# Part one of a streaming conformer layer: the order in which VectorE, ScalarE and GpSimd issue, and the lag before one attention head

## The chip, the cores and the metric

The kernel runs on one core of a Trainium2 chip. TensorE (PE) multiplies matrices, VectorE (DVE), ScalarE (ACT) and GpSimd (POOL) do the work on vectors, and SyncE (SP) issues most of the transfers between the chip's memory and the on-chip buffers. Each engine works through its own list of instructions, one after the other, and an instruction that waits for a semaphore holds everything behind it on that engine. The metric is the time of one execution on the device in microseconds; lower is better.

## The reference

One layer of a streaming encoder for 2048 prompt rows and 64 sample rows of width 1024:

```python
h = rms_norm(x, g1) * (1 + sc1) + sh1          # sc1, sh1, ... from silu(c) @ w_ada
z = h @ w_in                                    # glu_a | glu_b | q | k | v | two gates
u = glu_a * sigmoid(glu_b)
y = silu(layer_norm(causal_depthwise_conv(u, 31 taps) + b_dw))
conv_out = y @ w_conv_out
q, k = rms_norm(q per head), rms_norm(k per head)
o = softmax(q k^T / 8 + rel_bias, band of 9 chunks of 64) v      # 8 heads of 64
merged = sigmoid(g_conv) * conv_out + sigmoid(g_attn) * (o @ w_attn_out)
x = x + gt1 * (merged @ w_o)
x = x + gt2 * ffn(rms_norm(x, g2) * (1 + sc2) + sh2)             # SwiGLU, width 2816
```

The outputs are the new rows of prompt and sample, the last rows of the convolution's input, and the last k and v rows.

## The kernel before

The work is in two parts. Part one makes everything up to the attention's output and the gates; part two merges the two branches, adds the residual and does the feed-forward network. Only part one is touched here. It goes over the 2112 rows in four blocks (0 to 576 with the sample rows, then three of 512), and for each block through the stages in `ORDER`: q, first quarter of the convolution (GLU and taps), k, second quarter, v, third and fourth quarter, gates. A product in float32 precision is made as three matmuls of a high and a low half (`mm3`), so most operands exist twice: ACT rounds the high half (`whi`, `hh`, `ph`, `part_h`), DVE or POOL subtracts it to get the low half (`wlo`, `hl`, `pl`, `part_l`).

Beside the main stage, other work is fed in by a planner. Each piece (a block's conv-norm, a quarter's 31 taps, a tile's input norm, a head of attention) is a Python generator in a `Lane`; a `Meter` around every engine adds an estimate of each instruction's duration to that engine's load, and after each product `stream.spend()` lets lanes whose due time has come emit their next step. A step yields the load at which its inputs should be there. So the program's text order, as emitted, already is a plan for every engine. Which of it the chip sees is settled afterwards: the framework's scheduler puts each engine's instructions in an order of its own, except on the engines that are named in `tc.manual_schedule(...)`, which issue in the emitted order. Before, that was PE alone, from the end of the first block's opening products (`first_block`) to `ordered.close()` at the end of part one. Transfers that SP issues are in nobody's fixed list, so the scheduler places them in both kernels.

Every instruction of PE, DVE, ACT and POOL goes through `Meter.run`, so nearly all rows of the profile say L105 and are told apart by the names of their tiles:

- A head of attention (`attend`): `sc` (scores, PE, in one pair of PSUM banks), `pr,sm<-sc,bias` (score and maximum, DVE; the maximum is read by a following row `sm`), exp and scale of `pr` (ACT), transposes `ptp` (PE), `ph` (ACT) and `pl` (DVE), product with the values `po` (PE), `other` (ACT) and `o32_p` (DVE; the profile shortens it to `o_p`). The first block interleaves each prompt head with a head of the sample rows.
- Outputs kept as two halves (`parts()`): tiles `part_h` and `part_l`, two buffers each, shared by q and k after their norms, by conv-norm (`c_d`) and by attention output (`o_d`). A buffer comes free when the transfer that stores it has landed.
- Conv-norm of a block (`conv_norm`): POOL multiplies `y<-y,s`, ACT makes tanh `ln<-y,lnh`, DVE scales `y` and `ln`, then `part_h`, `part_l` and the two stores to `c_d`, four times per block of rows.
- q and k rows (`qk_rows`): `sq`, `kn` (ACT), `ssq`, `t` (DVE), `r` (POOL), `kn<-kn,r` (DVE), then transposes and `part_h`, `part_l`.

`fetch(i)` loads what head number i needs: q and k (`q2`, `kk`, one buffer each, so a head's load waits for the last scores of the head before) and the bias of the head. The head's first scores are due when the load meter of PE has moved on by a lag: `QK_LAG` = 9000 or, for a head that follows another kind of head, `FIRST_LAG` = 14000 ns. In each block the order of heads is 0 to 7; the heads of the first block are of kinds 0 and "s" in turn, those of the others of kind 1, 2 or 3.

Of the kernel before, what the change touches and what calls it, by code (L numbers as in the profile page):

```python
# [622 lines left out]
def streaming_layer(ctx: ExitStack, tc: tile.TileContext, I, O):  # L623
# [481 lines left out]
    def cached_kv():  # L1105
        rows_ = [(src, j) for j in range(CACHE // P) for src in (ck, cv)]
        ts = []
        for i, (src, j) in enumerate(rows_):
            for src_, j_ in rows_[len(ts) : i + 2]:
                t = temp("cache")  # L1110
                nc.sync.dma_start(t, src_[j_ * P : (j_ + 1) * P])
                ts.append((t, stream.load["pe"] + CACHE_LAG))
            t, landed = ts[i]
            yield landed
            if src is ck:
                store_kq(t, P, k_d, j * P)
            else:
                store_v(t, P, j * P)
            yield
# [349 lines left out]
    def load_bias(h):  # L1469
        for r in (0, HD):  # L1470
            nc.sync.dma_start(
                bias[r : r + HD, HD - r : 640 - r],
                bass.AP(tensor=rb_d.tensor, offset=rb_d.offset + 768 * h + HD, ap=[[1, HD], [1, 576]]),
            )
        return bias

    ahead_qk, spare = {}, {"open": False, "heads": []}
    order, loaded, now = [], {}, {"scored": -1, "finished": -1, "bias": None}
# [8 lines left out]
    def fetch_qk(i):  # L1487
        if i < len(order) and ("qk", i) not in now:
            x, h = order[i]
            if spare["open"]:  # L1490
                spare["heads"].append(i)
            now["qk", i] = load_qk(x, h, *spans(x))

    def fetch(i):
        if i < len(order) and i not in loaded:
            x, h = order[i]
            fetch_qk(i)
            if now["bias"] is None or now["bias"][0] != h:
                now["bias"] = h, load_bias(h)
            first = x != "s" and (not i or order[i - 1][0] not in (x, "s"))  # L1500
            lag = FIRST_LAG if first else QK_LAG
            loaded[i] = max(stream.load["pe"] + BIAS_LAG, ahead_qk.get(i, stream.load["pe"] + lag))

# [5 lines left out]
    def attend(i):  # L1509
        x, h = order[i]  # L1510
        q0, nq, k0, nk = spans(x)
        yield lambda: now["scored"] == i - 1
        fetch(i)
        fetch_v(i)
        if not i:
# [7 lines left out]
        for t in range(0, nq, P):  # L1523
            n = min(P, nq - t)
            if x not in (0, "s"):
                ps = ps_a.tile([P, 2, 512], F32, tag="s", name="sc")
                for j in range(2):
                    for d in range(2):
                        pe.matmul(ps[:, j, :320], q2[:, d, t : t + P], kk[:, t + 320 * j : t + 320 * j + 320], start=d == 0, stop=d == 1)
                w, src, bs = 640, ps[:, :, :320], bias[:, ::-1]  # L1530
            else:
                w = nk if x == "s" else t + P

                if "banks" not in now:
                    sc = ps_a.tile([P, 2, 512], F32, tag="s", name="sc")
                    now["banks"] = [sc[:, 0:1], sc[:, 1:2]]
                ps = now["banks"].pop(0)
                now["banks"].append(ps)
                for d in range(2):
                    pe.matmul(ps[:n, 0, :w], q2[:, d, t : t + n], kk[:, :w], start=d == 0, stop=d == 1)  # L1540
                src, bs = ps[:n, 0:1, :w], bias[:n, 64:384][:, ::-1] if x == "s" else bias[:, :w][:, ::-1]
            pr, sm, free, ready = softmax_max(src, n, w, bs)
            tiles.append((pr, sm, n, w))
            if t + P < nq:
                yield free + PE_LAG, SCORE_ROOM
            else:
                fetch(i + 1)
                if (x, order[min(i + 2, len(order) - 1)][0]) in ((0, 0), ("s", "s")):
                    fetch_qk(i + 2)
                now["scored"] = i  # L1550
            if t:
                softmax_scale(*tiles[-2], x in ON_ACT)
# [86 lines left out]
    W = Weights((nc.sync, act, dve, gps), wpool, dram, stream, list(weight_order()), source, 3, 5, lambda key: key[0] in KEPT)  # L1639
    first_block(xs)  # L1640
    ordered = ExitStack()
    ordered.enter_context(tc.manual_schedule(engines={mybir.EngineType.PE}))
    norm_lane.add(cached_kv())
    mods = mod_steps()
    norms = {}
# [734 lines left out]
```

## Time and profile before

| | |
|---|---|
| time, median of three runs | 2958.93 us (2955.85 to 2965.5) |
| the profiled execution's own time | 2957.35 us |
| its span, first to last instruction | 2955.5 us |
| mean granted TensorE clock | 0.995 |
| first block's opening products | 0 to 97 us |
| the stretch that the change can reorder | 97 to about 1181 us |
| part two | about 1181 to 2955.5 us |

In the rows that follow, a timeline row has the start and the duration in us, the engine, the operation with its tiles, and in brackets how long the engine was idle just ahead of it and who ended that. In a table by windows each engine has its busy time and, in parentheses, its number of instructions; then come the granted TensorE clock (1.00 is full speed), the busy share of the sixteen DMA engines and the bytes moved per time.

### The profile page before, as it was taken

To read this page: it belongs to the slowest core of one execution; us is meant where nothing else is said; L and a number is where in the kernel's file an instruction comes from. 1 tells how busy PE (TensorE), PEld (TensorE's weight loads), DVE (VectorE), ACT (ScalarE), POOL (GpSimd) and SP (SyncE) were. 2 spreads that over 40 slices of the span, in tenths; PEclk is the share of its full clock that TensorE was granted. 3 is DMA by queue.
4 is the path that set the end of the run, shared out by engine and by line. 5 is a ranking of instruction groups with operands and counts; after the bars stand their busy time and mean duration, and the time that the engine had idled before them with its cause. 6 is when DMAs were issued, how large, how long until landed. Compare 5 with 4: busy or idle time off the path is not lost.

```text
span 2955.5 us, 44837 instructions
## 1 busy us (share of the span) xinstructions
PE 2892.0 (98%) x16193; PEld 2586.7 (88%) x16193; DVE 2049.8 (69%) x3648; ACT 1364.3 (46%) x2453; POOL 1161.4 (39%) x753
## 2 busy tenths in 40 slices
PE   7999999999999999999999999999999999999999
PEld 5899777887888788888999998999999999999998
DVE  5897787668857885477777756666666547566666
ACT  3345533661465267464334345444444345444442
POOL 1101210111011102454666452366667742465767
PEclk9999999999999999999999999999999999999999
DMA  9989899878996897985444876232333965333333
GB/s 320 312 297 309 274 283 324 269 229 294 285 313 209 294 264 239 290 298 171 147 147 143 268 257 227 93 120 91 114 122 104 331 225 185 97 99 108 115 106 126
DMA packets 467067, 628.04 MB, mean 212 GB/s; under 512 B 36196, under 2 KB 314584, under 8 KB 466845
## 3 DMA queue, kind: packets, MB, share of 16 engines
q1 hardware_dynamic: 452944, 606.11, 63.4%
q10 hardware_dynamic: 13901, 19.08, 1.9%
q8 instruction: 127, 2.08, 0.3%
q14 instruction: 95, 0.78, 0.1%
HBM read 476.53 MB, written 148.54 MB: 211 GB/s over the span
## 4 chain that ended last, share of the span: by engine, by line
PE 46%; DVE 2%; DMA 2%; ACT 1%; issue 1%; POOL 1%; SPq 0%; ACTq 0%; DVEq 0%; POOLq 0%
PE ps L105 28%; PE pd L105 13%; PE pw L105 5%; DVE wlo L105 1%; DMA cin<-o_d 1%; ACT whi L105 1%; POOL wlo L105 0%; DMA tg<-g_d 0%; DVE ps L105 0%; ACT xn L105 0%; DMA wst<-in_w_ffn_in 0%; DMA wfo<-in_w_ffn_out 0%; DVE acc L105 0%; DVE sums L105 0%; PE pt L105 0%
## 5 line engine op out<-in xcount | busy, mean ns | idle before, releaser
L105 PE MATMUL ps<-t,whi 128*128 128x384 f32 (+1 forms) x2112 | 501.9, 322 | 3.2 <-DVE u L105 1.1
L105 POOL TENSOR_TENSOR wlo<-wst,whi 128x1024 fp32r<-128x1024 f32 (+1 forms) x159 | 362.7, 2293 | 233.7 <-ACT whi L105 195.6
L105 ACT ACTIVATE whi<-wst 128x1024 fp32r<-128x1024 f32 (+1 forms) x265 | 258.2, 979 | 316.5 <-PE ps L105 127.1
L105 PE MATMUL ps<-b,whi 128*128 128x384 f32 (+1 forms) x1584 | 380.6, 325 | 5.4 <-DVE v L105 2.1
L105 PEld LDWEIGHTS ps<-t,whi 128*128 128x128 f32 x2112 | 367.8, 188 | 10.6 <-ACT u L105 3.1
L105 DVE SCALAR_TENSOR_TENSOR y<-u,wd,y 128x512 f32<-128x512 f32 (+1 forms) x480 | 370.1, 773 | 7.5
L105 PE MATMUL ps<-hh,whi 128*128 128x512 f32 (+2 forms) x992 | 363.4, 366 | 0.1
L105 DVE TENSOR_TENSOR acc<-acc,pd 128x512 f32<-128x512 f32 x482 | 322.3, 685 | 48.7 <-PE pd L105 46.0
L105 PE MATMUL ps<-hh,wlo 128*128 128x512 f32 (+2 forms) x992 | 345.6, 348 | 0.3 <-DVE wlo L105 0.3
L105 PE MATMUL ps<-hl,whi 128*128 128x512 f32 (+2 forms) x992 | 345.2, 348 | 0.0
L105 PE MATMUL ps<-t,wlo 128*128 128x384 f32 (+1 forms) x1056 | 338.2, 321 | 0.0
L105 PE MATMUL pd<-whi,hid 128*128 128x512 f32 x912 | 297.5, 391 | 0.3 <-DVE hid L105 0.3
L105 PEld LDWEIGHTS ps<-b,whi 128*128 128x128 f32 x1584 | 276.8, 188 | 13.6 <-DVE v L105 3.2
L105 ACT ACTIVATE pr<-pr,sm 128x640 f32<-128x640 f32 (+2 forms) x272 | 202.1, 749 | 153.9 <-DVE sm L105 150.9
L105 PE MATMUL ps<-b,wlo 128*128 128x384 f32 (+1 forms) x792 | 256.0, 323 | 0.0
L105 POOL TENSOR_TENSOR r<-t,mhalf 128x1 f32<-128x1 f32 (+2 forms) x68 | 82.4, 1219 | 414.8 <-DVE t L105 375.0
L105 PEld LDWEIGHTS ps<-hh,wlo 128*128 128x128 f32 x992 | 187.3, 189 | 23.3 <-DVE wlo L105 0.5
L105 DVE TENSOR_TENSOR wlo<-wst,whi 128x1024 fp32r<-128x1024 f32 (+1 forms) x106 | 135.7, 1284 | 99.2 <-ACT whi L105 98.2
L105 PEld LDWEIGHTS ps<-hh,whi 128*128 128x128 f32 x992 | 187.7, 189 | 18.0 <-issue 2.9
L105 PEld LDWEIGHTS pd<-whi,hid 128*128 128x128 f32 x912 | 171.1, 188 | 36.5 <-DVE acc L105 0.8
L105 PEld LDWEIGHTS ps<-hl,whi 128*128 128x128 f32 x992 | 188.1, 190 | 14.5 <-issue 1.7
L105 PEld LDWEIGHTS ps<-t,wlo 128*128 128x128 f32 x1056 | 198.0, 188 | 0.8
(233 smaller groups left out, 6299.1 us busy)
## 6 DMA issues: line engine op xcount, KB each, us to landing
whi<-w_din_h SPq DMA_DIRECT2D x72, 512.0 KB, 5.2
wlo<-w_din_l SPq DMA_DIRECT2D x72, 512.0 KB, 7.8
wst<-sum_d SPq DMA_DIRECT2D x131, 256.0 KB, 2.9
wfo<-in_w_ffn_out SPq DMA_DIRECT2D x64, 512.0 KB, 4.1
wmod<-in_w_ada SPq DMA_DIRECT2D x46, 512.0 KB, 9.1
sum_d<-ws SPq DMA_DIRECT2D x88, 256.0 KB, 2.2
wst<-in_w_ffn_in SPq DMA_DIRECT2D x85, 256.0 KB, 3.2
wst<-in_w_in SPq DMA_DIRECT2D x40, 512.0 KB, 7.2
```

What stands on the lines that cost most here:

```text
L105: self.last = f(*args, **kw)
```

## The change

Two things. `fetch` gives the longer lag also to the first head of the block of kind 1, which follows the last sample head; before, only kinds 2 and 3 and the very first head had it. And the engines that issue in the emitted order in part one are now PE, DVE, ACT and POOL; SP stays with the scheduler.

```diff
-            first = x != "s" and (not i or order[i - 1][0] not in (x, "s"))
+            first = not i or x not in ("s", 0, order[i - 1][0])
             lag = FIRST_LAG if first else QK_LAG
...
-    ordered.enter_context(tc.manual_schedule(engines={mybir.EngineType.PE}))
+    ordered.enter_context(tc.manual_schedule(engines={mybir.EngineType.PE, mybir.EngineType.DVE, mybir.EngineType.Activation, mybir.EngineType.Pool}))
```

No instruction is added or removed on any engine. Three places show how rows move. Names carry the tile's number, so that tiles of one kind can be told apart.

First ACT at about 297 to 306 us, where the first block's heads meet the conv-norm of the sample rows (`ln_3480`, `part_h_3529`) and an attention output (`part_h_3610`). Before:

```order
L105 ACTIVATE pr_3519,sm_3520<-pr_3519,sm_3520 64x320
L105 ACTIVATE pr_3519<-pr_3519,sm_3520 64x320
L105 ACTIVATE gate_3569<-ps_3493 128x288
L1362 DMA g_d_68<-gate_3569 128x288
L105 ACTIVATE other_3588<-po_3385 64x512
L105 ACTIVATE hh_195<-h32_3471 128x4x128
L105 ACTIVATE hh_195<-h32_3508 128x4x128
L105 ACTIVATE gate_3617<-ps_3572 128x288
L1362 DMA g_d_68<-gate_3617 128x288
L105 ACTIVATE ph_3655<-ptp_3654 128x128
L105 ACTIVATE hh_195<-h32_3644 128x4x128
L105 ACTIVATE ph_3655<-ptp_3654 64x64
```

The next row there is `part_h_3529<-ln_3480`. On the same engine, after:

```order
L105 ACTIVATE pr_3519,sm_3520<-pr_3519,sm_3520 64x320
L105 ACTIVATE part_h_3529<-ln_3480 128x64
L105 ACTIVATE pr_3519<-pr_3519,sm_3520 64x320
L105 ACTIVATE gate_3569<-ps_3493 128x288
L1362 DMA g_d_68<-gate_3569 128x288
L105 ACTIVATE other_3588<-po_3385 64x512
L105 ACTIVATE part_h_3610<-o32_p_3137 128x512
L105 ACTIVATE gate_3617<-ps_3572 128x288
L1362 DMA g_d_68<-gate_3617 128x288
L105 ACTIVATE hh_195<-h32_3471 128x4x128
L105 ACTIVATE hh_195<-h32_3508 128x4x128
L105 ACTIVATE ph_3655<-ptp_3654 128x128
```

`part_h_3529` has moved from behind the `ph` rows to a place ahead of the scale of `pr_3519`, and `part_h_3610` ahead of them too.

Second DVE at about 351 to 364 us, the conv-norm of the first block's 512 prompt rows (`ln_4098` to `ln_4122`, stored from `part_l_4103`, `4111`, `4119`, `4127`), two tiles of q (`kn_4027` and `kn_4095`) and the score row of a head (`pr_4219,sm_4220`). Before:

```order
L105 TENSOR_TENSOR kn_4095<-kn_4095,r_4166 128x512
L105 TENSOR_SCALAR y_776<-y_776,cols_175 128x512 x2
L105 TENSOR_SCALAR ln_4098<-ln_4098,y_776 128x512
L105 TENSOR_SCALAR ln_4106<-ln_4106,y_776 128x512
L105 TENSOR_SCALAR y_776<-y_776,cols_175 128x512
L105 TENSOR_TENSOR part_l_4103<-ln_4098,part_h_4102 128x512
L105 TENSOR_SCALAR ln_4114<-ln_4114,y_776 128x512
L105 TENSOR_SCALAR y_776<-y_776,cols_175 128x512
L105 TENSOR_SCALAR ln_4122<-ln_4122,y_776 128x512
L105 TENSOR_TENSOR o32_p_4198<-other_4199,po_3906 64x512
L105 ISA pr_4219,sm_4220<-sc_1921,bias_194 128x128
L105 ISA sm_4220 128x1
```

On DVE, after:

```order
L105 TENSOR_SCALAR y_776<-y_776,cols_175 128x512
L105 TENSOR_SCALAR ln_4114<-ln_4114,y_776 128x512
L105 TENSOR_TENSOR part_l_4119<-ln_4114,part_h_4118 128x512
L105 TENSOR_SCALAR y_776<-y_776,cols_175 128x512
L105 TENSOR_SCALAR ln_4122<-ln_4122,y_776 128x512
L105 TENSOR_TENSOR part_l_4127<-ln_4122,part_h_4126 128x512
L105 TENSOR_SCALAR part_l_4152<-pt_4146,gqk_179,part_h_4151 128x512
L105 TENSOR_TENSOR kn_4027<-kn_4027,r_4041 128x512
L105 TENSOR_REDUCE ssq_4094<-sq_4093 128x8
L105 TENSOR_SCALAR t_4165<-ssq_4094 128x8
L105 TENSOR_TENSOR o32_p_4198<-other_4199,po_3906 64x512
L105 ISA pr_4219,sm_4220<-sc_1921,bias_194 128x128
```

Before, one of the five `part_l` rows (`part_l_4103`) stood ahead of the score row `pr_4219`; now all five do. On ACT all five `part_h` rows now stand ahead of the exp of `pr_4219`, and before only two did. On POOL the row `r_4041` (of q) now stands ahead of the four products `y<-y,s`; before it stood behind them.

Third PE at about 465 us, where the second block's first head begins (`sc` from `kk_5187`). Before:

```order
L105 MATMUL pa_5223<-sel_193,R_5240 128x128 x2
L105 MATMUL ps_5244<-hh_195,whi_5054 128x512
L105 MATMUL ps_5244<-hl_196,whi_5054 128x512
L105 MATMUL ps_5244<-hh_195,wlo_5055 128x512
L105 MATMUL sc_5297<-kk_5187,q2_5186 128x320 x4
```

On PE, after:

```order
L105 MATMUL ps_5308<-hh_195,wlo_5085 128x512
L105 MATMUL ps_5308<-hh_195,whi_5084 128x512
L105 MATMUL ps_5308<-hl_196,whi_5084 128x512
L105 MATMUL ps_5308<-hh_195,wlo_5085 128x512
L105 MATMUL sc_5337<-kk_5187,q2_5186 128x320 x4
```

The head's first scores stand 24 matmuls (eight products) further down, in the next product's accumulation (`ps_5308`). The head's four groups of scores then stand closer together, its last one five products further down than before; between that and the first scores of the next head (`kk_5422` before, `kk_5448` after) stand 13 products now, and before 11 with four groups of transposes (`ptp`) and a pair of `po`, `pa` rows. From the end of the second block on, PE's rows stand as before.

## Prediction

> **What bounds the kernel now.** I read the page first: the span, the engines' busy time and the chain that ended last.
>
> ```profile
> span 2955.5 us, 44837 instructions
> PE 2892.0 (98%) x16193; PEld 2586.7 (88%) x16193; DVE 2049.8 (69%) x3648; ACT 1364.3 (46%) x2453; POOL 1161.4 (39%) x753
> PE 46%; DVE 2%; DMA 2%; ACT 1%; issue 1%; POOL 1%; SPq 0%; ACTq 0%; DVEq 0%; POOLq 0%
> ```
>
> PE is busy 98% of the span, and no other engine has more than 2% of the chain. A change of order on DVE, ACT and POOL can therefore only move the times at which PE waits, and the time it spends at a lower clock. Next, the same by stretches; the change reaches 97 to 1181 us.
>
> ```profile
> 97.00:314.00 217.00, 211.59 (x1432) 198.10 (x1431) 183.21 (x330) 102.94 (x218) 30.20 (x32) 0.99 0.88 301
> 314.00:403.00 89.00, 80.06 (x404) 63.84 (x403) 72.04 (x152) 44.73 (x95) 23.53 (x18) 0.94 0.89 289
> 403.00:499.00 96.00, 90.38 (x505) 71.60 (x505) 70.66 (x143) 32.50 (x71) 5.38 (x8) 0.98 0.93 300
> 499.00:1181.00 682.00, 674.16 (x3665) 568.87 (x3664) 504.18 (x965) 356.80 (x644) 84.78 (x71) 1.00 0.84 268
> ```
>
> Columns: length, busy time of PE, PEld, DVE, ACT and POOL, then PE's clock, the DMA share and GB/s. PE's idle time is 5.4, 8.9, 5.6 and 7.8 us, so 27.8 us in all is the most that better order could give at full clock, and 14.5 of it lies between 314 and 499. Past 499 PE idles 1% of the time. Who ends the idle time, from the waits of PE over 97 to 1181 (total, times, longest):
>
> ```profile
> PE sc L105 <- DVE sm L105: 11.7, 8, 5.7
> PE sc L105 <- DMA kk<-k_d: 4.6, 2, 4.3
> PE pt L105 <- DVE u L105: 1.9, 1, 1.9
> PE pt L105 <- ACT whi L105: 1.6, 1, 1.6
> PE pa L105 <- DMA wmod<-in_w_ada: 1.3, 2, 0.7
> ```
>
> Scores that wait for the maximum of the scores before (`sm`, on DVE) are the largest item, then one load of keys. A long wait also costs clock:
>
> ```profile
> 310.50:313.90 3.40, 3.40 (x17) 3.40 (x16) 2.06 (x8) 3.36 (x11) 1.69 (x2) 0.50 1.03 374
> 392.40:402.70 10.30, 7.68 (x24) 6.58 (x25) 8.76 (x21) 3.28 (x10) 0.21 (x1) 0.50 0.94 331
> 494.80:498.30 3.50, 3.30 (x9) 2.88 (x10) 0.21 (x1) 0.00 (x0) 0.00 (x0) 0.51 0.53 138
> ```
>
> At clock 0.50 half of PE's busy time is lost: 1.7 us, 3.8 us and 1.65 us. Each stretch follows one of PE's three long waits (2.86, 5.70 and 4.29 us, quoted below).
>
> [...]
>
> **The change, part by part.** No instruction is added or taken away, so every term is a wait that moves. I go by places.
>
> *ACT at 298 us.* The row `part_h<-ln` (128x64), which stood behind `ph`, now stands ahead of the 64x320 scale of `pr`. Its buffer is the one whose store SP issued at 298.50:
>
> ```profile
> 298.50 0.50 SPq L1348 DMA_DIRECT2D c_d<-part_h  x1
> c_d<-part_h SPq DMA_DIRECT2D x1, 32.0 KB, 6.0
> 298.21 0.56 ACT L105 ACTIVATE pr<-pr,sm 64x320 f32<-64x320 f32 x1 [0.22 <-DVE sm L105]
> 303.12 0.28 ACT L105 ACTIVATE ph<-ptp 128x128 fp32r<-128x128 f32 x1 [1.58 <-PE ptp L105]
> 304.99 0.20 PE L105 MATMUL po<-ph,vv 128*128 128x64 f32 x1
> 309.31 0.50 PE L105 MATMUL sc<-kk,q 128*128 128x256 f32 x2 [2.86 <-DVE sm L105]
> ```
>
> 298.5 + 6.0 = 304.5: ACT is held from 298.2 until then. Queued behind are the scale, a gate, `other`, `part_h` of the attention output, two `hh` and the `ph` that PE needs; in rows of 0.28 to 0.63 us they end near 309, and `pl` on DVE follows, so `po` moves from 304.99 to about 309.2. The 2.86 us wait at 309.31 lies behind it and takes up part: the scores come at about 311.9. Net +2.6 us on PE; bounds 0 (the store lands earlier) and +4.2 (nothing absorbed). The half clock that follows stays as it is.
>
> *DVE, ACT and POOL at 341 to 363 us.* All five pairs `part_h`, `part_l` now stand ahead of the score row that ran at 357.24, and they share two buffers.
>
> ```profile
> 344.96 0.60 ACT L105 ACTIVATE sq<-ps 128x512 f32<-128x512 f32 x1 [4.98 <-PE ps L105]
> 341.29 4.90 POOL L105 TENSOR_TENSOR y<-y,s 128x512 f32<-128x512 f32 x4 [4.42 <-DVE s L105]
> 349.39 1.64 POOL L105 TENSOR_TENSOR r<-t,mhalf 128x8 f32<-128x8 f32 x1 [1.61 <-DVE t L105]
> 345.94 2.93 ACT L105 ACTIVATE ln<-y,lnh 128x512 f32<-128x512 f32 x4
> 353.31 0.63 ACT L105 ACTIVATE part_h<-ln 128x512 fp32r<-128x512 f32 x1 [4.45 <-DVE ln L105]
> 353.97 0.32 SPq L1348 DMA_DIRECT2D c_d<-part_h  x1
> 354.25 0.68 DVE L105 TENSOR_TENSOR part_l<-ln,part_h 128x512 fp32r<-128x512 f32 x1
> 357.24 0.28 DVE L105 CUSTOM_DVE_ANT_0 pr<-sc,bias 128x128 f32<-128x128 f32 x1
> c_d<-part_l SPq DMA_DIRECT2D x2, 256.0 KB, 2.0
> 357.57 0.51 PE L105 MATMUL sc<-kk,q 128*128 128x256 f32 x2 [0.92 <-DVE sm L105]
> ```
>
> POOL's `y<-y,s` must now wait for `r`: `sq` 344.96 + 0.6, `ssq` and `t` some 0.9 (estimates by DVE rows of like size, 0.68), `r` 1.64 make 348.1, the first product 1.2 more (4.90 / 4), tanh 0.7 (2.93 / 4), two DVE rows 1.3: the first `part_h` at about 351.3. That is earlier than 353.31, since DVE no longer does `kn` first. From there a buffer turns over in `part_h` 0.63, `part_l` 0.7, issue 0.3, landing 2.0 = 3.6 us; the fifth pair is two turns behind the first: 351.3 + 7.2 = 358.5, plus its own pair 1.3, `kn`, `ssq`, `t` and `o_p` about 2.2, and the score row 0.3: 362.3 instead of 357.5. I take +5.0 us, the value so worked out, rounded up, because the landing of 2.0 us is the nearest row and already the shortest; the low end is 0 (stores of the fourth and fifth pair land sooner and DVE does them in idle time), the high end +11 (each store meets the 6.0 us landing of the row at 298.50: two turns of 7.6 instead of 3.6 us give 8 more, less the earlier start). A wait of over 5 us brings a half-clock stretch like the one at 310.50: +1.7.
>
> *DVE at 388 to 395 us.*
>
> ```profile
> 390.37 0.69 DVE L105 TENSOR_TENSOR kn<-kn,r 128x512 f32<-128x512 f32 x1 [1.53 <-POOL r L105]
> 394.68 0.27 DVE L105 CUSTOM_DVE_ANT_0 pr<-sc,bias 128x128 f32<-128x128 f32 x1
> 395.01 0.79 PE L105 MATMUL sc<-kk,q 128*128 128x256 f32 x2 [5.70 <-DVE sm L105]
> ```
>
> This `kn`, with the 1.53 us that DVE idles for it, two `pl` and one tap now stand behind the score row, which so can run about 3.5 us sooner. PE arrives 9.3 us later (2.6 + 5.0 + 1.7), DVE some 5 later less those 3.5, so the whole wait of 5.70 goes: 9.3 − 5.7 = +3.6 behind it. The long half-clock stretch goes with it (−3.8), but DVE is still the engine that PE follows here (72.0 of 89.0 us busy), and I leave one short stretch of 1.7 in: +1.5 us in all at 403. Bounds: −9.5 (no hold at 298 and 357, wait and clock both gone) and +9.6 (the high hold with its stretch, 2.6 + 11 + 1.7, less the 5.7).
>
> *The lag, 465 to 500 us.*
>
> ```profile
> 490.09 0.39 PE L105 MATMUL ps<-hl,whi 128*128 128x512 f32 x1
> 490.31 0.40 PE L105 MATMUL ps<-hh,wlo 128*128 128x512 f32 x1
> 495.00 1.40 PE L105 MATMUL sc<-kk,q 128*128 128x320 f32 x4 [4.29 <-DMA kk<-k_d]
> 484.94 0.45 SPq L1428 DMA_DIRECT2D kk<-k_d  x1
> kk<-k_d SPq DMA_DIRECT2D x2, 256.0 KB, 10.8
> 441.00:494.00 53.00, 48.39 (x285) 37.72 (x283) 39.98 (x76) 16.64 (x33) 3.42 (x6) 1.00 1.00 332
> ```
>
> The keys of the second block's second head land 10.8 us after their issue because the DMA engines are full (share 1.00 for 53 us): what is ahead in the queues decides, not the moment of issue. With the first head's scores moved five products down (15 matmuls 0.23 us apart, two `sc` groups less and a `pa` more, about +4 in all, and the wait for the modulation), PE wants the keys at about 495 instead of 490.7, and they land at about 495 either way. So I take the whole 4.29 and its 1.65 of clock off, and add 1 for the modulation's loads in front, which PE now reaches earlier while the queues are as full: −5.0. Bounds: −6 (nothing added) and +2 (the load, issued 4 us later, lands 4 us later, and PE waits as before and for the modulation too).
>
> *The other waits*, 1.9 and 1.6 us and less: the rows ahead of `u` and of `whi` are the same set, and elsewhere holds of one row (0.3 to 1.1 us) arise and go. I cost them at 0 and allow −4 to +4. Behind 499 us PE has 7.8 us of idle time in 682, so DVE, ACT and POOL run ahead of it, which is the cover; where a conv-norm's five pairs hold a score row again, it would cost as at 357.
>
> Sum: +1.5 − 5.0 + 0 = −3.5 against this execution's own 2957.35, so 2953.9. The median of the runs is 1.6 higher than that execution, so I forecast 2955. About 0.3% (8.9 us) is what can be told from no change, and −3.5 is inside it.
>
> **The rivals.**
>
> *Slower: the two buffers of `part_h` and `part_l` become the bound in conv-norm.* In the emitted order each of the four conv-norms puts its pairs ahead of score rows. For it: the 6.0 us landing at 298.50, and a DMA share of 0.89 in that stretch. Against it: landings of 2.0 us at 353, and the spare time of DVE past 499 (504 of 682 us busy). Price: +9.6 at 403, the high end above, less the lag's 5.0 is +4.6; a hold of 5.0 with its 1.7 of clock in one later block makes +11.3, in two +18: 2957.35 plus these and the 1.6 gives 2964, 2970 and 2977. It decides once a pair's turn is above 6 us. I name 2970.
>
> *Faster: the holds are covered.* If the stores land in 2.0 us everywhere and PE's matmuls in front of the held scores last, 298 and 357 cost nothing, 395 gives 5.7 + 3.8, the lag 5: −14.5, so 2944. For it: the score row at 357.24 itself waited behind rows that go. Against it: the two-turn count above.
>
> *Nothing: DVE is the engine that PE follows at 360 to 395, whatever its order, and the keys at 495 wait for the queues.* The holds then are swallowed by the 5.70 us wait, half clock stays, and the lag gives nothing because the modulation's waits take it: 2959 to 2961.
>
> **How the numbers follow.** My sum, as worked out (2949 to 2960): 0.40, predicted 2955. Slower: 0.30 (2964 to 2978). Faster: 0.18 (2940 to 2949). Nothing: 0.12 (2957 to 2963). The sum's own range is 2949 to 2960; for 8 in 10, both other signs count: 2942 to 2974. Under 2950.0 lie the faster rival and a sixth of the sum's: 0.25. Above 2967.8 lie most of the slower rival and a little of the sum's high end: 0.27. The rest, 0.48, is within 0.3%.
>
> **What would show it.** Right: a wait of `ptp` or `po` for ACT near 300 to 305; ACT's `part_h` idle on a transfer of `c_d` near 358, with PE's `sc` waiting for `sm` there by 5 us or so; no wait over 2 us near 395 to 400 and clock 1.00 there; no wait for `kk` at the second block's second head. Wrong: waits of `sc` for `sm` of several us past 499, at conv-norm of the later blocks (then the slower rival); a wait for `kk` of 4 us at about 495 (then the lag bought nothing); no wait near 357 at all (then the faster one).

## The result and the profile after

The changed kernel takes 3012.16 us (median of four runs, 3010.72 to 3013.62) against 2957.39 before: a ratio of 1.0177, 95% interval 1.0165 to 1.0189. It is slower by about 52 us, where 2955 was forecast with a range up to 2974. The page of the changed kernel, in the three lines that were shown of before:

```profile
span 3011.2 us, 44879 instructions
PE 2912.7 (97%) x16193; PEld 2586.4 (86%) x16193; DVE 2049.2 (68%) x3648; ACT 1358.9 (45%) x2453; POOL 1164.3 (39%) x753
PE 46%; DVE 2%; ACT 1%; DMA 1%; issue 1%; POOL 0%; ACTq 0%; DVEq 0%; SPq 0%
```

The engines do the same work (2049 us on DVE in both; the 42 instructions more are all semaphore instructions), PE is still the bound, and the chain of work that ended last looks as before. PE's idle time has grown from 63.5 to 98.5 us (span less busy), and its busy time by 20.7 us for the same instructions. To see where, I took the start of the same product's matmul in both traces (products keep their sequence) and subtracted; the difference is called the lateness:

| in the trace before, us | later after the change, us |
|---|---|
| 101 | −0.2 |
| 294 | +16.9 |
| 355 | +19.3 |
| 365 | +27.3 |
| 406 | +26.0 |
| 490 | +26.4 |
| 500 | +18.7 |
| 602 | +25.4 |
| 800 | +38.6 |
| 1004 | +44.7 |
| 1181 | +58.5 |
| 1254 | +57.3 |

The loss is not at one place. It is 17 us before 294, 8 us near 360, and some 40 us that creep in between 500 and 1181, the stretch that the prediction took for covered; only near 495 is something won. The waits of PE over the same stretch of the program, 97 to 1235 us:

```profile
PE sc L105 <- DVE sm L105: 28.0, 29, 6.7
PE ptp L105 <- ACT pr L105: 9.5, 12, 1.5
PE pt L105 <- DVE kn L105: 3.9, 5, 1.3
PE ps L105 <- DVE hl L105: 3.9, 3, 1.9
PE po L105 <- DVE pl L105: 2.2, 5, 1.1
```

Scores wait for `sm` 29 times instead of 8, and the transposes of the probabilities for ACT 12 times, 9.5 us, instead of 0.7 us in two (a row of the same view of before). After the second block's first heads, 526 to 1239 us, by windows and by waits:

```profile
526.00:1239.00 713.00, 684.15 (x3649) 564.15 (x3647) 499.00 (x964) 351.40 (x642) 86.09 (x73) 1.00 0.81 256
PE sc L105 <- DVE sm L105: 8.3, 19, 1.1
PE ptp L105 <- ACT pr L105: 6.9, 8, 1.5
```

Before, the same products ran from 506.5 to 1181 us, 674.5 us in all, with 7.8 us of idle time on PE; now there are 28.9 us of it, in waits of which none is over 2 us. PE's busy time there grew as well, by 17.5 us (666.7 to 684.2), of which the slow stretch at 678.80 below explains some 1.7 (an estimate: half of its 3.30 us, by the clock of 0.50). Part of the rest looks like waiting that the profile books as busy: a row `sc` is booked with 0.41 us in the mean behind a wait and with 0.31 us without one. That the remainder is waits too short to show as idle is an inference: a matmul's booked time reaches into the next one (`ps<-hh,whi`: 0.40 us booked, 0.24 us from start to start). In the same stretch of before, scores waited for `sm` 1.5 us in three times. Half clock adds to it; the slow stretches after the change (PE's clock is the value behind the engines' columns):

```profile
187.20:190.60 3.40, 3.40 (x15) 3.40 (x16) 3.29 (x5) 1.65 (x4) 0.00 (x0) 0.50 1.03 402
221.30:224.70 3.40, 3.40 (x16) 3.30 (x16) 1.41 (x5) 1.10 (x4) 0.00 (x0) 0.50 1.04 390
337.40:340.80 3.40, 3.40 (x9) 2.65 (x8) 0.00 (x0) 1.38 (x3) 2.15 (x2) 0.50 1.11 259
378.40:388.60 10.20, 6.02 (x39) 3.15 (x39) 5.86 (x17) 4.36 (x12) 1.85 (x2) 0.50 0.89 288
419.40:429.50 10.10, 9.13 (x27) 7.70 (x28) 8.01 (x21) 3.76 (x12) 1.80 (x2) 0.50 0.98 342
678.80:682.10 3.30, 3.30 (x11) 2.81 (x10) 2.77 (x8) 2.41 (x5) 0.00 (x0) 0.50 0.49 142
```

That is 33.8 us at half clock where before had 17.2 in this part. In the stretch at 678.80 two `ps` matmuls of 128x512 start 0.43 us apart (678.82 and 679.25), and at clock 1.00 it is 0.23 (1115.11 and 1115.34).

**What DVE and ACT wait for.** The largest rows of DVE's and ACT's waits over 97 to 1181 us, first of the kernel before:

```profile
DVE pl L105 <- ACT ph L105: 44.4, 61, 4.4
...
DVE part_l L105 <- ACT part_h L105: 11.6, 12, 4.1
...
ACT pr L105 <- DVE sm L105: 150.9, 148, 8.3
```

and of the changed one:

```profile
DVE pl L105 <- ACT ph L105: 94.3, 81, 3.1
DVE part_l L105 <- ACT part_h L105: 32.2, 28, 4.8
...
ACT pr L105 <- DVE sm L105: 277.5, 150, 10.3
```

DVE waits for ACT at `pl` twice as long, ACT waits for DVE at the exp (`pr<-pr,sm`) nearly twice as long. (The changed kernel stands at the same product at 1239 us; to there its wait at `pl` is 110.3 us.) How one becomes the other shows at 1111 to 1117 us, in the timelines of DVE, ACT and PE of the changed kernel:

```profile
1111.38 0.82 DVE L105 CUSTOM_DVE_ANT_0 pr<-sc,bias 128x640 f32<-128x640 f32 x1
1112.12 0.08 DVE L105 DVE_READ_ACCUMULATOR2_ANT sm<- 128x1 f32 x1
1113.68 1.29 DVE L105 TENSOR_TENSOR pl<-ptp,ph 128x512 fp32r<-128x512 f32 x2 [1.48 <-ACT ph L105]
1114.88 0.74 DVE L105 SCALAR_TENSOR_TENSOR y<-u,wd,y 128x512 f32<-128x512 f32 x1
1115.54 0.81 DVE L105 CUSTOM_DVE_ANT_0 pr<-sc,bias 128x640 f32<-128x640 f32 x1
...
1112.24 0.83 ACT L105 ACTIVATE pr<-pr,sm 128x640 f32<-128x640 f32 x1 [3.57 <-DVE sm L105]
1113.07 1.06 ACT L105 ACTIVATE ph<-ptp 128x512 fp32r<-128x512 f32 x2
...
1111.28 0.60 PE L105 MATMUL ptp<-ident,pr 128*128 128x128 f32 x4
1112.42 0.74 PE L105 MATMUL sc<-kk,q 128*128 128x320 f32 x4
1116.42 0.41 PE L105 MATMUL sc<-kk,q 128*128 128x320 f32 x1 [0.70 <-DVE sm L105]
```

ACT sits idle for 3.57 us at an exp that needs `sm`; the `ph` behind it has its transposes by 1111.9 but comes at 1113.07. DVE then sits idle for 1.48 us at `pl`, which needs `ph`; behind `pl` stand a tap that needs nothing and the next score row, whose scores are there at about 1113.2. So the next `sm` comes at 1116.4 and PE waits. The kernel before had the same pair of exp and `ph` at that place, but DVE put a tap into the gap and the next `pl` only then:

```profile
1062.83 0.75 DVE L105 SCALAR_TENSOR_TENSOR y<-u,wd,y 128x512 f32<-128x512 f32 x1
...
1064.39 0.69 DVE L105 TENSOR_TENSOR pl<-ptp,ph 128x512 fp32r<-128x512 f32 x1 [0.33 <-ACT ph L105]
...
1066.20 0.81 DVE L105 CUSTOM_DVE_ANT_0 pr<-sc,bias 128x640 f32<-128x640 f32 x1
```

The score row at 1066.20 starts 1.1 us behind the first of its scores (1065.06 on PE), and PE goes on to the next scores at 1068.09 without a wait; in the changed kernel it starts 3.1 us behind them (1112.42 to 1115.54).

The theory formed from this (C): the emitted rows of DVE and ACT hand waits to each other, and it takes both to be rigid, because the scheduler can arrange either one around the other. Its rivals: DVE's row alone (A), ACT's alone (B), POOL's row, the lag, and a plan that takes DVE for faster than it is (P).

### The profile page after: what moved, and what is told of

Read it like the earlier page. It is cut to its first block, busy times and chain, and to the rows that moved or that the text cites. A ratio compares the mean times of both kernels' runs of the same rounds, so it can differ in the third digit from the quotient of the medians.

```text
span 3011.2 us, 44879 instructions
## 1 busy us (share of the span) xinstructions
PE 2912.7 (97%) x16193; PEld 2586.4 (86%) x16193; DVE 2049.2 (68%) x3648; ACT 1358.9 (45%) x2453; POOL 1164.3 (39%) x753
## 4 chain that ended last, share of the span: by engine, by line
PE 46%; DVE 2%; ACT 1%; DMA 1%; issue 1%; POOL 0%; ACTq 0%; DVEq 0%; SPq 0%
PE ps L105 28%; PE pd L105 13%; PE pw L105 4%; DVE wlo L105 1%; DVE ps L105 0%; ACT whi L105 0%; DMA tg<-g_d 0%; DMA cin<-o_d 0%; ACT xn L105 0%; DMA wfo<-in_w_ffn_out 0%; DVE sums L105 0%; PE pt L105 0%; ACT t L105 0%; DMA x<-x_d 0%; DVE acc L105 0%
## 5 line engine op out<-in xcount | busy, mean ns | idle before, releaser
L105 PEld LDWEIGHTS ps<-t,whi 128*128 128x128 f32 x2112 | 367.7, 188 | 10.2 <-ACT u L105 3.3
```

Source lines behind the costliest of these rows:

```text
L105: self.last = f(*args, **kw)
```

## The experiments

Losses in us are the ratio to the kernel before, less one, times 2960, with the interval's ends.

**Parts of the change.** `lag_only` has the first edit alone, `order_only` the second alone; the others name fewer engines in `manual_schedule`, with the lag as before:

```diff
-    ordered.enter_context(tc.manual_schedule(engines={mybir.EngineType.PE}))
+    ordered.enter_context(tc.manual_schedule(engines={mybir.EngineType.PE, mybir.EngineType.DVE}))
```

Only the lag:

> Only the lag of the second block's first head is changed; the engines' order stays as before. The prediction's term for the lag says -5 us: 2950 to 2954, no wait for kk near 495. If the lag is part of the loss, it is slower by 5 us or more. If the queues swallow it, 2956 to 2960.

All three engines, without the lag:

> Only the emitted order on DVE, ACT and POOL, with the short lag. If the loss is made of many short holds of the emitted order, nearly all of the 55 us is here: 3008 to 3020, with waits of PE for sm, pr and pl in every block. If the lag makes a large part of the loss, it is below 2990.

DVE alone, then ACT alone:

> DVE alone issues in the emitted order beside PE. Theory A (DVE's row is what holds: pl waits for ph on ACT, and the taps and score rows behind it wait too, so ACT waits for sm): 2985 to 3015, with DVE's wait for ph near 90 us and ACT's for sm well above 151. Theory B (ACT's row is what holds: part_h and whi stand ahead of exp and scale): 2955 to 2970. Theory C (it takes both): under 2980 here and under 2980 with ACT alone, the two losses adding up to much less than 55.

> ACT alone issues in the emitted order beside PE. Theory A: 2955 to 2970. Theory B: 2985 to 3015. Theory C: under 2980.

DVE and ACT, then POOL alone:

> DVE and ACT issue in the emitted order beside PE, POOL with the scheduler, lag as before. Theory C (hand-over: each of the two holds the other, and only where the scheduler may mend neither): 3005 to 3020, nearly the whole 60 us of all three engines, where DVE alone lost 18 and ACT alone 4. If POOL's row carries the rest, 2975 to 2990 (18 + 4).

> POOL alone issues in the emitted order beside PE. Theory C: 2955 to 2965, within 5 us of the kernel before. If POOL's row carries the rest of the loss, 2985 to 3000.

| kernel | median, us | ratio to before (95%) | loss, us |
|---|---|---|---|
| lag only | 2953.07 | 0.9978 (0.9968 to 0.9989) | −6.5 (−9.5 to −3.3) |
| DVE, ACT, POOL | 3019.93 | 1.0206 (1.0185 to 1.0226) | 61 (55 to 67) |
| DVE alone | 2978.29 | 1.0061 (1.0045 to 1.0077) | 18 (13 to 23) |
| ACT alone | 2964.30 | 1.0016 (1.0007 to 1.0025) | 4.7 (2.1 to 7.4) |
| DVE and ACT | 3017.94 | 1.0191 (1.0176 to 1.0206) | 57 (52 to 61) |
| POOL alone | 2962.32 | 1.0004 (0.9994 to 1.0013) | 1 (−2 to 4) |

The lag is a gain, and the loss is all in the order (61 less 6.5 is about the changed kernel's 52). DVE and ACT together lose 57 us, and their single losses add up to only 23: so it does take both, as theory C says, and A and B each fall. POOL adds nothing that can be told. With DVE alone fixed, DVE waits at `pl` still 86.6 us (111.0 with all three engines fixed), and ACT's wait for `sm` does not grow; the waits of DVE and of ACT in that kernel (97 to 1240 us):

```profile
DVE pl L105 <- ACT ph L105: 86.6, 87, 4.8
...
ACT pr L105 <- DVE sm L105: 147.8, 111, 8.0
```

**The wait at `pl`, first try.** The low half of a prompt head's probabilities is made from the transposed tile and a constant, without `ph`; in both kernels, so that the loss can be taken against the same edit.

```diff
-                    split(ph[:, t0 * P :], pl[:, t0 * P :], pt[:, t0 * P :])
+                    act.activation(ph[:, t0 * P :], pt[:, t0 * P :], AF.Copy)
+                    stream.after("dve", "act")
+                    by = lambda a: a[:, t0 * P :].rearrange("p (a b) -> p a b", b=P)
+                    dve.tensor_tensor(by(pl), by(pt), ident.unsqueeze(1).to_broadcast([P, w // P, P]), ALU.subtract)
```

> All three engines in the emitted order, lag as before, but the low half of a prompt head's probabilities is made from the transposed tile and a constant instead of from ph, so pl no longer waits for ACT (pl is then not the low half). PE's order is the same. Theory C with pl as the way from ACT to DVE: the loss against the same edit in the kernel before falls from 60 to 30 us or less. If pl's wait only fills time in which DVE would wait for something else, the loss stays above 45 us.

> The kernel before with the same edit of pl (pl is then not the low half). Both theories: 2945 to 2962, as PE is busy 98% and the scheduler already puts other rows ahead of pl.

The two kernels took 3014.38 and 2960.76 us, a loss of 53 us. This tells nothing of the theory, since the wait was still there. DVE's waits over 97 to 1240 us with this edit:

```profile
DVE pl L105 <- ACT ph L105: 108.1, 86, 4.9
```

That is hardly less than the 111.0 us without the edit, though these `pl` rows read nothing that ACT writes. They do still read the transposed tile, which ACT reads too; the next edit, which leaves that tile out, has 5.3 us of this wait left.

**The wait at `pl`, taken away.** `pl` is now made from a constant alone, `ident` less `ident`.

> All three engines in the emitted order, lag as before. The low half of a prompt head's probabilities is now made from a constant alone (pl is zero), since an edit that still read the transposed tile still waited for ACT, which reads the same tile. PE's order is the same. If DVE's wait at pl is what makes its later rows late, the loss against the same edit in the kernel before is 35 us or less instead of 59. If it is not (DVE would wait at the next row instead, or is late because taps stand ahead of score rows), the loss stays above 45 us.

> The kernel before with the same edit (pl is zero): 2945 to 2962 by both.

The result is 2990.48 us, ratio 1.0103 (1.0087 to 1.0118), against 2961.22 us, 1.0005 (0.9995 to 1.0015): 29 us are left of 61. So about half of the loss is DVE's wait at `pl`, in a kernel where ACT's row is fixed too. The lateness, taken for these kernels as in the table above, shows that this is the half that creeps in: from 600 to 1181 us the kernel with all three engines falls behind by 37 us (29.0 to 66.2), and with the wait taken away by 12 (23.1 to 34.9). Of DVE's wait at `pl` for ACT 5.3 us are left, at the heads of the sample rows, which the edit does not touch; the other waits of DVE for ACT stay:

```profile
DVE part_l L105 <- ACT part_h L105: 44.0, 31, 5.4
DVE o_p L105 <- ACT other L105: 42.1, 21, 4.6
...
DVE pl L105 <- ACT ph L105: 5.3, 11, 1.6
```

**The planner's costs.** A tap (`scalar_tensor_tensor`) of 512 columns is planned with 607 ns on DVE and takes 773 in the mean of the page's group.

```diff
-            ns = 75 + n * (8.3 if op == "reciprocal" else 0.75 if fast else 1.04)
+            ns = 75 + n * (8.3 if op == "reciprocal" else 0.75 if fast else 1.36 if op == "scalar_tensor_tensor" else 1.04)
```

> All three engines in the emitted order, lag as before, but the planner charges a tap of 512 columns 771 ns on DVE instead of 607 (measured: 773 in the mean). This moves the plan of all engines, PE too. Theory P (the emitted order is bad because the plan takes DVE for faster than it is, so that score rows stand behind taps that are not done in time): the loss against the kernel before with the same costs falls from 59 to 30 us or less. Theory C (the two rigid rows hand waits to each other whatever the costs): it stays above 45 us.

> The kernel before with the same cost of taps, only PE in the emitted order: both theories 2945 to 2975, as PE's plan is only spread a little.

The two kernels took 3026.43 and 2979.58 us: with these costs the order loses 47 us. That is less than 61, but far from 30, so the tap's cost, the only one that was corrected, does not make the whole loss. It does seem to matter early: between these two kernels the lateness grows by 4 us up to 294 us, where it was 19 with the old costs, and by some 26 from 500 to 1181 us, where it was 39. This is one trace of each, and PE's plan has moved as well. The kernel before loses 19 us (1.0064, 1.0045 to 1.0082) with the truer cost, and so lies above the 2975 that was named.

**The rest of the loss.** DVE alone with `pl` from a constant; and all three engines with `pl`, 74 of the 76 `part_l` rows and `o_p` from a constant, so that none of these rows waits for ACT's result (the attention output and the low halves are then zero), against the same edit before:

```diff
-        dve.tensor_tensor(o32[mine, :n], t[mine, :n], po[mine, :n], ALU.add)
+        flat(o32[mine, :n])
...
-            name = low(hi[:, :n], lo[:, :n], tmp[:, :n], n, TT_LESS)
+            stream.after("dve", "act")
+            flat(lo[:, :n])
+            name = "dve"
```

> Only DVE in the emitted order beside PE, and pl made from a constant (pl is zero). DVE alone lost 18 us. If what DVE alone loses is its wait at pl, 2955 to 2965. If it is the place of taps ahead of score rows, 2972 to 2982 as before the edit.

> All three engines in the emitted order, and beside pl also the low halves part_l (of q, k, conv-norm and attention output) and o_p are made from a constant, so that none of these DVE rows waits for ACT (these values are then zero, the attention output too). If the other half of the loss is DVE's waits for ACT at these rows, the loss against e15 is 12 us or less. If it comes from ACT's waits for DVE or from taps ahead of score rows, it stays at 22 to 32 us.

> The kernel before with the edit of e14: 2940 to 2962 by both.

DVE alone stays at 2977.81 us, a loss of 18 as before the edit: where ACT's row is left to the scheduler, the wait at `pl` costs nothing that shows, however long DVE waits there. All three engines come to 2981.05 against 2967.36 us (the edit by itself costs the kernel before 6 us; 2962 was the highest named): 14 us are left, by the two intervals 8 to 19, just above the 12 that were named and under 22. So another 16 us or so (8 to 23) are DVE's waits for ACT at `part_l` and `o_p`. What remains, 14 us, is about what DVE alone loses, and it falls in the same place: against the same edit before, the lateness is 15.7 us at 365 and 13.6 at 1181, and in DVE's own kernel it is 9.7 at 200, 17.4 at 365 and 18.5 at 1181. That taps and conv-norm rows stand ahead of score rows there would fit, but no run took these rows apart.

**A later place for `pl`.** The plan emits `pl` a step after `ph`, when ACT's load says that `ph` is done.

```diff
-                    split(ph[:, t0 * P :], pl[:, t0 * P :], pt[:, t0 * P :])
+                    act.activation(ph[:, t0 * P :], pt[:, t0 * P :], AF.Copy)
+                    yield stream.when("act")
+                    dve.tensor_tensor(pl[:, t0 * P :], pt[:, t0 * P :], ph[:, t0 * P :].bitcast(F32), ALU.subtract)
```

> All three engines in the emitted order, lag as before; the plan emits pl not together with ph but at its next step after ACT's load says that ph is done; pl's wait itself is kept, nothing is left out, and PE's plan moves a little. If the place of emission makes half the loss, 2985 to 3000. If the costs that the plan works with place it as badly later, 3010 to 3030.

The kernel took 3019.36 us, ratio 1.0198 (1.0182 to 1.0213), so nothing is gained: the place that the plan holds for right is not the right one on the chip.

The lag alone, 2953.07 us, is faster than both kernels, by 0.2% than the one before.

## Why the prediction was wrong

**The step that failed** is "the other waits": "I cost them at 0 and allow −4 to +4. Behind 499 us PE has 7.8 us of idle time in 682, so DVE, ACT and POOL run ahead of it, which is the cover". Those stretches lost 17 us before 294 and 40 after 500. PE's small idle time there was no cover that DVE and ACT had whatever their order; it was there as long as the scheduler ordered at least one of the two rows, as at 1063 us, where it put a tap between `sm` and `pl`. With either row fixed the loss is 18 or 5 us, with both 57, and DVE's idle time at `pl` grew from 44 to 94 us. The waits of DVE for ACT make some 47 of the 61 us. I looked at each engine's new order with the others at their old times, and so could not see a wait that goes round.

**The slower rival** had the sign but not the mechanism: it expected one or two more holds by the two buffers of `part_h` in later conv-norms, 2964 to 2977. In the later blocks the waits of scores for `sm` are 19 of at most 1.1 us, and the transfers to `c_d`, by whose landing these buffers come free, hold ACT 0.3 us and DVE 0.9 us in the whole of 97 to 1239 us.

**ACT at 298 us: +2.6 expected; the hold is not there,** though this stretch lost 2.4 (16.9 to 19.3), which is luck. `part_h` ran without any wait; the stores to `c_d` ahead of it, issued at 309.83 and 310.99, landed 2.3 us after their issue in the median:

```profile
312.40 0.56 ACT L105 ACTIVATE pr<-pr,sm 64x320 f32<-64x320 f32 x1 [0.24 <-DVE sm L105]
...
313.00 0.26 ACT L105 ACTIVATE part_h<-ln 128x64 fp32r<-128x64 f32 x1
```

PE's wait of 2.86 us at 309.31 in the trace before and its slow stretch, on which the step counted, are gone (lateness 12.7 at 314). A wait of PE for `wlo` on POOL (2.16 us at 337.09) and the slow stretch at 337.40 came in their place.

**DVE, ACT and POOL at 341 to 363 us: +6.7 expected with its clock, +8.0 measured** (19.3 to 27.3). The place and the wait are as forecast, the turn of the buffers is not. On ACT, DVE and PE of the changed kernel:

```profile
366.62 0.82 ACT L105 ACTIVATE ln<-y,lnh 128x512 f32<-128x512 f32 x1
369.12 0.63 ACT L105 ACTIVATE part_h<-ln 128x512 fp32r<-128x512 f32 x1 [1.68 <-DVE ln L105]
369.65 0.80 ACT L105 ACTIVATE ln<-y,lnh 128x512 f32<-128x512 f32 x1
371.85 0.63 ACT L105 ACTIVATE part_h<-ln 128x512 fp32r<-128x512 f32 x1 [1.39 <-issue]
...
369.78 0.69 DVE L105 TENSOR_TENSOR part_l<-ln,part_h 128x512 fp32r<-128x512 f32 x1 [0.70 <-ACT part_h L105]
372.51 0.69 DVE L105 TENSOR_TENSOR part_l<-ln,part_h 128x512 fp32r<-128x512 f32 x1 [0.75 <-ACT part_h L105]
382.24 0.28 DVE L105 CUSTOM_DVE_ANT_0 pr<-sc,bias 128x128 f32<-128x128 f32 x1
...
382.58 0.58 PE L105 MATMUL sc<-kk,q 128*128 128x256 f32 x1 [6.67 <-DVE sm L105]
```

A pair takes 2.73 us (369.12 to 371.85) where half of 3.6 was forecast, not by its buffer (only the fifth pair waits for transfers to `c_d`, 0.35 and 0.92 us) but because `ln`, `y`, `ln`, `part_h`, `part_l` go back and forth between the two engines with nothing between: the same hand-over as at the heads, which I had in view at this place and did not look for elsewhere. The start was misread too: the `r` that now stands ahead of `y<-y,s` is that of the first tile of q, whose `t` in the trace before was done by 343.9, and not the one behind `sq` at 344.96. So the forecast started 1.5 us too late (351.3, against 369.12 − 19.3 = 349.8) and turned too fast, and its score row at 362.3 came close to 382.24 − 19.3 = 362.9 by luck. PE's wait was 6.67 us, and half clock held for 10.2 us, of which PE was busy 6.0: half of that, 3.0 us, is what it cost by the clock (an estimate), where I had charged 1.7. The high end of this hold, +11, takes the earlier start off twice; by its own terms it is +13.

**DVE at 388 to 395 us: −7.8 expected** (from +9.3 to +1.5), **−1.3 measured** (27.3 to 26.0). The wait shrank but stayed, and with it the whole slow stretch of 10.1 us quoted above:

```profile
420.37 0.58 PE L105 MATMUL sc<-kk,q 128*128 128x256 f32 x1 [3.68 <-DVE sm L105]
```

**The lag: −5.0 expected, −6.5 (−9.5 to −3.3) measured** with the lag alone, and the products near 500 us come 7.7 us sooner in the changed kernel, against the lateness at 490 (26.4 to 18.7). The wait for the keys is nearly gone with the lag alone:

```profile
PE sc L105 <- DMA kk<-k_d: 0.6, 1, 0.6
```

There the two loads of keys are issued 3.2 and 1.9 us later than before (485.51 and 486.81) and land 7.4 us after their issue in the median, where it was 10.8. So a later issue did not make the keys land later, as the step said; that the queues held them was its estimate, from the DMA share of 1.00 over 441 to 494 us.

## What to carry to other kernels

Two engines that pass tiles back and forth can lose far more when both are held to an order that was planned ahead of time than when either is (57 us here, against 18 and 5), even where a third engine is busy 98% and seems to cover them: idle time that a scheduler has filled looks like cover in the profile before. To judge such a change, follow a wait round the loop (score row, exp, high half, low half, next score row) instead of moving one engine's rows against the others' old times. A change of two parts should be tried in its parts: here the lag alone is worth 6.5 us.

## What the runs showed of the hardware

Half clock came behind a short wait too, and not behind every longer one. A wait of 1.13 us at 220.45 was followed by 3.4 us at clock 0.50 (221.30 to 224.70, above):

```profile
220.45 0.30 PE L105 MATMUL po<-pl,vv 128*128 128x64 f32 x1 [1.13 <-DVE pl L105]
```

A wait of 1.92 us in the trace before (`pt` for `u`, until 987.1) was followed by none (clock 1.00 over 900 to 1000 us), and neither was one of 1.52 us in the changed kernel (`ptp` for `pr`, until 1149.0; clock 1.00 over 1100 to 1250 us). So the length of the wait alone does not decide in these two traces; what does, no run here tells.
